# Reordering block products in a one-core hybrid layer: P2 moved ahead of P6

## The chip, the core and the metric

The kernel runs on one core of one Trainium2 chip. The metric is the device time of one execution in microseconds (us): the median of three runs before the change was 349.57 us (348.91 to 350.58). Profiled times come from one further execution, which the hardware profiler recorded.

Engines are called by the profile's names: PE does matmuls, PEld loads the stationary operand of a matmul, DVE is the vector engine, ACT the scalar engine, POOL the third elementwise engine (which here also starts some transfers), SP the engine that starts most transfers.

## The reference

One layer over 256 tokens of width 1024, batch 1. After a modulated RMS norm, one wide projection gives thirteen pieces: attention queries, keys, values and gate (`qa, ka, va, za`), the same for a recurrent memory (`qm, km, vm, zm, om` and two small gates), and two output gates:

```
h = _rmsnorm(x, norm_w) * (1 + scale) + shift
(qa, ka, va, za, qm, km, vm, zm, om, ig, fg, ga, gm) = jnp.split(h @ w_in, SPLIT_IDX, axis=-1)
ya = (ya * jax.nn.silu(za)) @ w_att_proj
hm = jax.nn.sigmoid(heads(om, ML_HEADS)) * hm
ym = (merge(hm) * jax.nn.silu(zm)) @ w_ml_proj
y = jax.nn.sigmoid(ga) * ya + jax.nn.sigmoid(gm) * ym
return x + gate * (y @ w_out)
```

Only four of the projections matter here: `vm` (the memory's values), `om` (its output gate), `zm` and `ga`. Each is a product of the 256x1024 matrix h with a 1024x1024 piece of `w_in`. Every order in which they are computed gives the same values.

## The kernel before, in words

**Matmul in three passes.** Every fp32 operand is split into a high part and a low rest, and each product is three matmuls: high by high, high by low, low by high. For the weights `split` (from L508) does it for one group at a time: ACT casts the raw weights to `wh` (L515), DVE subtracts to get `wl` (L519). Both live in rings of five buffers (`HB = 5`), and `split(g + 4)` is written in the loop turn of group g. So the cast of group g+4 has to wait until PE has finished group g-1, and ACT and DVE can be at most four groups ahead of PE.

**Groups.** PE works through a fixed list of groups, `place`. A whole group of `zm` (L1178 to L1180) is 12 matmuls 512 wide, a whole group of `ga` (L1185 to L1188) is 24 matmuls 256 wide. `zm` and `ga` have eight groups each, in two halves; `zm1.2` below is the third group of the second half.

**Block products.** `vm` and `om` are computed as 2x2 block matrices with seven products instead of eight (`PRODUCTS`, L51), in the order P1, P5, P3, P2, P6, P7, P4. Each product is two half groups of 6 matmuls 512 wide (L1161 to L1163). The seven products of one name share two banks of the accumulator memory (tiles called `aux`): P1, P2, P6 and P7 go to bank 0, P5, P3 and P4 to bank 1. Some add to what stands in the bank, some start it anew; P2 is added on top of P1, and **P6 starts bank 0 anew**. So whatever P2 completed has to be read out first:

- `ev_block(name, "P2")` calls `block_done(name, 0, 0, ...)`. For `om` that is one copy on ACT (L818, `omt<-aux`). For `vm` it is a cast on ACT (L822, `vaug<-aux`) and then a subtraction on DVE that reads the bank once more (L823, `vml<-aux,vaug`).
- P5 is copied out by ACT (L843), P6 by two instructions on DVE (L845, L846), P7 by two (L849, L850), P4 by one (L854); each of the last three is followed by a cast or a sigmoid on ACT (L822 or L818), and for `vm` by L823 on DVE.

These read-outs are written in the loop turn behind the last group of a product, after that turn's `split`. ACT and DVE do their work strictly in the order written, so a read-out stands behind the cast and the subtraction of the group four places ahead.

**Transfers.** The weights of a product come as a 1 MB block into one of seven raw buffers, started by SP as soon as a buffer is free. Products that need a sum of two weight blocks get the second block added by a transfer that accumulates, started by POOL three groups ahead (`block_sum`, L768).

**What sets the order.** The string `MIXED` (L54) is read letter by letter. V and O take the next product of `vm` and `om` (two half groups), z and g the next group of `zm` and `ga`. Nothing else is scheduled: the order of the instructions on each engine is the order in which the loop over `place` writes them:

```
pi = ended.get(g)
if g + A < NG:
    split(g + A, hooks_between.get(g, []))
    release(cons.get(g + A, []))
while pending:
    block_done(*pending.pop(0))
if block and pi != C["om", 6]:
    ev_block(chunks[pi]["name"], chunks[pi]["product"])
...
EV[pc["name"]](mmt[pi], pc["half"])
```

Groups are counted from the start of `place`; the first half group of `vm`'s P1 is 44.

Of the kernel before, what the change touches and what calls it, by code (L numbers as in the profile page):

```python
# [50 lines left out]
PRODUCTS = (("P1", (0, 0), 0, True), ("P5", (0, 0), 1, True), ("P3", (1, 1), 1, False), ("P2", (1, 0), 0, False),  # L51
            ("P6", (0, 0), 0, True), ("P7", (1, 1), 0, False), ("P4", (0, 0), 1, True))
BLOCK_SUMS = dict(P1=(0, 1), P5=(1, 1), P6=(1, 0), P3=(0, 1))
MIXED = "VzzzOzVzVzOVzVOzOOgVgOgVgOgggg"  # L54
W_PIECES = ((0, 512), (512, NR), (512, 1024), (1024, NR))


# [13 lines left out]
def tile_hybrid(ctx: ExitStack, tc: tile.TileContext, x, c, params2, w_row, w_va, ada_mod, ada_gate,  # L71
# [282 lines left out]
    for i, ch in enumerate(chunks):  # L354
        if ch["name"] == "ga" and ch["half"] == 0:
            whole = {name: [(C[name, hf], kp) for hf in range(2) for kp in range(4)] for name in ("ga", "zm")}
            whole.update({name: [(C[name, j], kp) for j in range(7) for kp in range(2)] for name in ("vm", "om")})
            for what in MIXED:
                name = dict(g="ga", z="zm", V="vm", O="om")[what]
# [895 lines left out]
```

## Time and profile before

| | before |
|---|---|
| median of 3 runs | 349.57 us |
| the profiled execution, its own time | 350.07 us |
| span from first to last instruction in it | 348.2 us |
| PE busy | 340.3 us (98%) |
| DVE busy | 276.8 us (79%) |
| ACT busy | 229.0 us (66%) |
| POOL busy | 84.5 us (24%) |

Busy time is the sum of an engine's instructions. A line of the timeline gives the start and the duration of an instruction in us from the start of the span, then engine, source line, operation, what it writes and reads, and, in brackets, how long its engine sat idle before it and which instruction released it. Matmuls are pipelined, so the next one starts well before the one before it has ended; how fast PE advances is read from one start to the next.

### The profile page before, as it was taken

Reading aid. Unit: us, or ns where it says so; the run is one execution under the profiler, and the core shown is the slowest. Engines: PE = TensorE matmul, PEld = TensorE weight load, DVE = VectorE, ACT = ScalarE, POOL = GpSimd, SP = SyncE. Lnnn points to the kernel's source line nnn. Section 1 sums busy time; section 2 is a strip of 40 time slices with the busy share of each in tenths; the row PEclk is TensorE's granted clock in tenths of the full one; section 3 lists DMA queues with packets and bytes.
Section 4 is the critical chain, followed back from the end, with each engine's and each line's share of the span. In section 5 each row is a group of like instructions: output and inputs, shape, how many; then the busy total and the mean of one; then the engine's idle time right before and its main releaser. Section 6 shows DMA issues by size and latency. Waiting matters only on the chain.

```text
span 348.2 us, 6229 instructions
## 1 busy us (share of the span) xinstructions
PE 340.3 (98%) x2408; PEld 318.3 (91%) x2408; DVE 276.8 (79%) x420; ACT 229.0 (66%) x355; POOL 84.5 (24%) x83
## 2 busy tenths in 40 slices
PE   7999999999999999999999999998999999999996
PEld 7787889999999999999998888777999999999995
DVE  5999996978995979776997778797796677759952
ACT  4868779799787676766747586675766554726410
POOL 4600002843201736554031332521000102000000
PEclk9999999999999999999999999999999999999999
DMA  7999999978481597283896999999997039160011
GB/s 267 420 414 413 418 417 422 311 285 354 148 337 62 179 361 253 70 320 151 284 266 176 232 149 256 263 242 262 391 350 272 0 124 360 64 243 0 2 60 62
DMA packets 30909, 84.09 MB, mean 241 GB/s; under 512 B 3224, under 2 KB 5152, under 8 KB 30240
## 3 DMA queue, kind: packets, MB, share of 16 engines
q1 hardware_dynamic: 26376, 74.78, 57.9%
q0 software_dynamic: 4352, 8.39, 13.9%
q10 hardware_dynamic: 152, 0.53, 0.4%
q8 instruction: 19, 0.31, 0.3%
q14 instruction: 10, 0.08, 0.1%
HBM read 82.43 MB, written 1.25 MB: 240 GB/s over the span
## 4 chain that ended last, share of the span: by engine, by line
PE 94%; DMA 2%; ACT 1%; DVE 1%; issue 1%; SPq 0%; ACTq 0%; DVEq 0%
PE mm L1187 15%; PE mm L1185 15%; PE mm L1188 15%; PE pm L202 13%; PE mm L1180 4%; PE mm L1179 4%; PE mm L1178 4%; PE aux L1161 4%; PE aux L1162 4%; PE aux L1163 4%; PE mm L1171 3%; DMA adat<-in_ada_mod_dram 2%; PE aux L671 1%; PE aux L709 1%; PE mm L1198 1%; PE mm L1200 1%
## 5 line engine op out<-in xcount | busy, mean ns | idle before, releaser
L519 DVE TENSOR_TENSOR wl<-raw,wh 128x1024 fp32r<-128x1024 f32 (+1 forms) x104 | 126.5, 1229 | 36.6 <-ACT wh L515 35.9
L515 ACT CAST wh<-raw 128x1024 fp32r<-128x1024 f32 (+1 forms) x112 | 112.1, 1017 | 31.2 <-PE mm L1187 15.1
L1185 PE MATMUL mm<-hTh,wh 128*128 128x256 f32 x320 | 90.0, 281 | 0.0
L1187 PE MATMUL mm<-hTl,wh 128*128 128x256 f32 x320 | 88.9, 278 | 0.0
L1188 PE MATMUL mm<-hTh,wl 128*128 128x256 f32 x320 | 88.9, 278 | 0.0
L1187 PEld LDWEIGHTS mm<-hTl,wh 128*128 128x128 f32 x320 | 60.4, 189 | 0.2
L1185 PEld LDWEIGHTS mm<-hTh,wh 128*128 128x128 f32 x320 | 60.1, 188 | 0.2
L1188 PEld LDWEIGHTS mm<-hTh,wl 128*128 128x128 f32 x320 | 60.2, 188 | 0.0
L768 POOL DMA_DIRECT2D raw<-in_w_in_dram x16 | 19.4, 1212 | 49.9 <-DVE wl L519 38.6
L1178 PE MATMUL mm<-wh,hTh 128*128 128x344 f32 (+1 forms) x80 | 28.0, 350 | 0.0
L1180 PE MATMUL mm<-wh,hTl 128*128 128x344 f32 (+1 forms) x80 | 27.7, 346 | 0.0
L1179 PE MATMUL mm<-wl,hTh 128*128 128x344 f32 (+1 forms) x80 | 27.7, 346 | 0.0
L519 POOL TENSOR_TENSOR wl<-raw,wh 128x1024 fp32r<-128x1024 f32 x8 | 20.0, 2527 | 15.8 <-ACT wh L515 15.8
L187 ACT CAST wrh<-raw 128x512 fp32r<-128x512 f32 (+1 forms) x24 | 18.2, 761 | 8.0 <-DMA raw<-in_w_row_dram 7.9
L192 DVE TENSOR_TENSOR wrl<-raw,wrh 128x512 fp32r<-128x512 f32 (+1 forms) x26 | 20.4, 812 | 1.1 <-ACT wrh L187 1.1
L202 PE MATMUL pm<-wrh,hTh 128*128 128x512 f32 x64 | 19.9, 392 | 0.4 <-ACT hTh L172 0.4
L202 PE MATMUL pm<-wrh,hTl 128*128 128x512 f32 x64 | 19.8, 391 | 0.0
L202 PE MATMUL pm<-wrl,hTh 128*128 128x512 f32 x64 | 19.0, 395 | 0.0
L1188 PE MATMUL mm<-yah,wl 128*128 128x256 f32 x64 | 17.7, 276 | 0.0
L1185 PE MATMUL mm<-yah,wh 128*128 128x256 f32 x64 | 17.7, 276 | 0.0
L1187 PE MATMUL mm<-yal,wh 128*128 128x256 f32 x64 | 17.7, 276 | 0.0
L1185 PE MATMUL mm<-ymh,wh 128*128 128x256 f32 x64 | 17.7, 276 | 0.0
(252 smaller groups left out, 773.4 us busy)
## 6 DMA issues: line engine op xcount, KB each, us to landing
raw<-in_w_in_dram SPq DMA_DIRECT2D x30, 1024.0 KB, 7.0
adat<-in_ada_mod_dram SPq DMA_DIRECT2D x16, 512.0 KB, 8.7
raw<-in_w_in_dram POOLq DMA_DIRECT2D x16, 512.0 KB, 8.5
raw<-in_w_va_dram SPq DMA_DIRECT2D x6, 688.0 KB, 9.3
raw<-in_ada_gate_dram SPq DMA_DIRECT2D x4, 1024.0 KB, 10.0
raw<-in_w_att_proj_dram SPq DMA_DIRECT2D x4, 1024.0 KB, 7.2
raw<-in_w_ml_proj_dram SPq DMA_DIRECT2D x4, 1024.0 KB, 7.2
raw<-in_w_out_dram SPq DMA_DIRECT2D x4, 1024.0 KB, 5.5
```

The lines of the kernel that those rows point to most:

```text
L187: copy(wsp[k][0][:, c0:c1], wrow[k][:, c0:c1])
L192: e.tensor_tensor(l[:, cs], wrow[k][:, cs], h[:, cs].bitcast(F32), op=OP.subtract)
L202: nc.tensor.matmul(pm[ch][:, t], a[:, k, t * 128:(t + 1) * 128], b[:, cs], start=k == 0 and i == 0, stop=k == KT - 1 and i == 2)
L515: nc.scalar.copy(h, w)
L519: e.tensor_tensor(l, w, h.bitcast(F32), op=OP.subtract)
L768: nc.gpsimd.dma_start(rawt[li][:, ks], w_block(ch["name"], *BLOCK_SUMS[ch["product"]])[:, ks], accum_op=OP.add)
L1178: nc.tensor.matmul(o, a, wh[:, kk], start=first, stop=False)
L1179: nc.tensor.matmul(o, a, wl[:, kk], start=False, stop=False)
L1180: nc.tensor.matmul(o, b, wh[:, kk], start=False, stop=last)
L1185: nc.tensor.matmul(o, wh[:, kk, cs], sh_[:, k], start=first and i % 2 == 0, stop=False, skip_group_check=True)
L1187: nc.tensor.matmul(o, wh[:, kk, cs], sl_[:, k], start=False, stop=False, skip_group_check=True)
L1188: nc.tensor.matmul(o, wl[:, kk, cs], sh_[:, k], start=False, stop=last and i % 2 == 1, skip_group_check=True)
```

## The change

Only the string that sets the order differs:

```diff
-MIXED = "VzzzOzVzVzOVzVOzOOgVgOgVgOgggg"
+MIXED = "VzzzOzVzVzVOzVOOzgOVgVgOgOgggg"
```

The groups that come out of it, from 58 on (before 58 and after 83 the two lists are the same; .0 and .1 are the two halves of a product):

| groups | before | now |
|---|---|---|
| 58, 59 | om P5 | vm P2 |
| 60, 61 | vm P2 | om P5 |
| 62 | zm1.2 | zm1.2 |
| 63, 64 | vm P6 | vm P6 |
| 65, 66 | om P3 | om P3 |
| 67 to 69 | zm1.3, om P2.0, om P2.1 | om P2.0, om P2.1, zm1.3 |
| 70 to 72 | om P6.0, om P6.1, ga0.0 | ga0.0, om P6.0, om P6.1 |
| 73, 74 | vm P7 | vm P7 |
| 75 | ga0.1 | ga0.1 |
| 76, 77 | om P7 | vm P4 |
| 78 | ga0.2 | ga0.2 |
| 79, 80 | vm P4 | om P7 |
| 81 | ga0.3 | ga0.3 |
| 82, 83 | om P4 | om P4 |

No instruction is added or taken away on PE, DVE, ACT, POOL or SP; they stand in another order. On PE, at the end of `om`'s P2 (its last three matmuls, which write the bank `aux_2314` from `hTh` and `hTl`), before, P6 writes the same bank next, from `hsum`:

```order
L1161 MATMUL aux_2314<-wh_2554,hTh_70 128x512
L1162 MATMUL aux_2314<-wl_2555,hTh_70 128x512
L1163 MATMUL aux_2314<-wh_2554,hTl_71 128x512
L1161 MATMUL aux_2314<-wh_2568,hsum_2206 128x512
L1162 MATMUL aux_2314<-wl_2569,hsum_2206 128x512
L1163 MATMUL aux_2314<-wh_2568,hsum_2206 128x512
```

and now the last group of `zm` follows (12 matmuls of which three are shown, then the 24 of ga0.0, and only then P6):

```order
L1161 MATMUL aux_2314<-wh_2542,hTh_70 128x512
L1162 MATMUL aux_2314<-wl_2543,hTh_70 128x512
L1163 MATMUL aux_2314<-wh_2542,hTl_71 128x512
L1178 MATMUL mm_2410<-wh_2554,hTh_70 128x512
L1179 MATMUL mm_2410<-wl_2555,hTh_70 128x512
L1180 MATMUL mm_2410<-wh_2554,hTl_71 128x512
```

Two whole groups have come between P2 and P6 on PE.

On ACT, which reads `vm`'s and `om`'s P2 out of the bank (L822 `vaug<-aux` and L818 `omt<-aux`; one `wh<-raw` is the cast of one group, L843 the read-out of `om`'s P5, L764 that of `zm`), from the middle of the stretch, before:

```order
L843 COPY omt<-aux 128x512
L515 CAST wh<-raw 128x1024 x2
L822 CAST vaug<-aux 128x2x256
L515 CAST wh<-raw 128x1024 x4
L822 CAST vaug<-vmt 128x2x256
L515 CAST wh<-raw 128x1024 x2
L764 ACTIVATE zmt<-mm 128x2x512
L515 CAST wh<-raw 128x1024 x2
L818 ACTIVATE omt<-aux 128x512
L515 CAST wh<-raw 128x1024 x3
L818 ACT_TABLE_LOAD
```

and now:

```order
L822 CAST vaug<-aux 128x2x256
L515 CAST wh<-raw 128x1024 x2
L843 COPY omt<-aux 128x512
L515 CAST wh<-raw 128x1024 x4
L822 CAST vaug<-vmt 128x2x256
L515 CAST wh<-raw 128x1024 x3
L818 ACTIVATE omt<-aux 128x512
L515 CAST wh<-raw 128x1024
L764 ACTIVATE zmt<-mm 128x2x512
L515 CAST wh<-raw 128x1024 x4
L818 ACT_TABLE_LOAD
```

The read-out of `vm`'s P2 comes two casts sooner, that of `om`'s P2 one cast sooner and ahead of `zm`'s; the table load ahead of `om`'s first sigmoid comes one cast later.

On DVE, from the read-out of P7 of `vm` on (L849, L850), before, `om`'s P7 (`omt`) goes ahead of `vm`'s P4 (L854 `vmt<-aux,vmt`):

```order
L849 TENSOR_TENSOR omt<-aux,omt 128x512
L850 TENSOR_TENSOR omt<-omt 128x512
L519 TENSOR_TENSOR wl<-raw,wh 128x1024 x3
L854 TENSOR_TENSOR vmt<-aux,vmt 128x512
L519 TENSOR_TENSOR wl<-raw,wh 128x1024
L823 TENSOR_TENSOR vml<-vmt,vaug 128x512
L519 TENSOR_TENSOR wl<-raw,wh 128x1024
L854 TENSOR_TENSOR omt<-aux,omt 128x512
```

and now it follows it:

```order
L854 TENSOR_TENSOR vmt<-aux,vmt 128x512
L519 TENSOR_TENSOR wl<-raw,wh 128x1024
L823 TENSOR_TENSOR vml<-vmt,vaug 128x512
L519 TENSOR_TENSOR wl<-raw,wh 128x1024 x2
L849 TENSOR_TENSOR omt<-aux,omt 128x512
L850 TENSOR_TENSOR omt<-omt 128x512
L519 TENSOR_TENSOR wl<-raw,wh 128x1024 x2
L854 TENSOR_TENSOR omt<-aux,omt 128x512
```

The two read-outs have changed places, with the subtractions of the weights around them shared out anew.

## The prediction

> **What bounds the kernel now.** I read the page's busy times and chain first, then the list of what PE waited for, and then the timeline of PE at the two waits that lie in the stretch the change touches.
>
> ```profile
> PE 340.3 (98%) x2408; PEld 318.3 (91%) x2408; DVE 276.8 (79%) x420; ACT 229.0 (66%) x355; POOL 84.5 (24%) x83
> PE 94%; DMA 2%; ACT 1%; DVE 1%; issue 1%; SPq 0%; ACTq 0%; DVEq 0%
> PE aux L1161 <- ACT omt L818: 1.8, 1, 1.8
> PE warm L231 <- POOL ident masks.py:199: 1.4, 1, 1.4
> PE xps L267 <- ACT diag L250: 0.7, 1, 0.7
> PE pm L202 <- ACT hTh L172: 0.4, 1, 0.4
> PE aux L1161 <- DVE vml L823: 0.3, 1, 0.3
> ```
>
> PE is busy for 98% of the span and makes up 94% of the chain that ended last. So only what makes PE stand still counts, and the list of its waits is short: three at the start, where nothing changes, and two on L1161, the first matmul of a block product. One waits for ACT's copy of `om`'s P2 (L818), the other for DVE's subtraction in the read-out of `vm`'s P2 (L823). These are the two P6 that must not start bank 0 anew before P2 has been read out of it.
>
> ```profile
> 220.37 0.39 PE L1163 MATMUL aux<-wh,hTl 128*128 128x512 f32 x1
> ...
> 223.09 0.39 PE L1180 MATMUL mm<-wh,hTl 128*128 128x512 f32 x1
> 223.77 0.50 PE L1161 MATMUL aux<-wh,hsum 128*128 128x512 f32 x1 [0.29 <-DVE vml L823]
> ...
> 226.62 0.39 PE L1161 MATMUL aux<-wh,hsum 128*128 128x512 f32 x1
> ...
> 234.55 0.39 PE L1163 MATMUL aux<-wh,hTl 128*128 128x512 f32 x1
> 236.70 0.50 PE L1161 MATMUL aux<-wh,hsum 128*128 128x512 f32 x1 [1.76 <-ACT omt L818]
> ...
> 239.57 0.28 PE L1185 MATMUL mm<-hTh,wh 128*128 128x256 f32 x1
> ...
> 242.40 0.40 PE L1161 MATMUL aux<-wh,hsum 128*128 128x512 f32 x1
> ```
>
> The rows are, in order: the last matmul of `vm`'s P2, the last of zm1.2, the first of `vm`'s P6, the first of `om`'s P3, the last of `om`'s P2, the first of `om`'s P6, the first of ga0.0, and the first of `vm`'s P7. Between 226.62 and 234.55 PE runs freely for 35 matmuls, so one takes (234.55 - 226.62) / 35 = 0.2266 us.
>
> **What the two waits cost.** From the last matmul of zm1.2 to the first of `om`'s P3 are 13 steps (12 matmuls of P6 lie between): 226.62 - 223.09 = 3.53 us against 13 x 0.2266 = 2.95, so 0.58 us are lost. From the last of `om`'s P2 to the first of ga0.0 are 13 steps too: 239.57 - 234.55 = 5.02 against 2.95, so 2.07 us. Together 2.65 us. The lower bound is the idle time alone that the rows in brackets show, 0.29 + 1.76 = 2.05 us: it leaves out that the bar of the last matmul runs on for 0.39 us where a free stream would have started the next after 0.23, and that the first matmul behind a wait takes 0.50 us. The upper bound is the idle time of the weight loads in the same stretch, which stood 2.2 and 0.7 us for the same two releasers:
>
> ```profile
> L1161 PEld LDWEIGHTS aux<-wh,hsum 128*128 128x128 f32 x12 | 2.2, 187 | 3.3 <-ACT omt L818 2.2 <-DVE vml L823 0.7
> ```
>
> That makes 2.9 us. I take 2.65, because only it counts from start to start. The Trainium skill (Trainium Kernel Development and Optimization, section Performance Expectations) calls matmul busy time a bad metric, since matmuls are pipelined, and names the busy share of LDWEIGHTS as a good one. By that rule the sum would be nearer to 2.9 than to 2.05; the trace agrees so far that the matmul bars of 0.39 us overlap at a spacing of 0.23.
>
> **Does the new order remove them?** The read-outs themselves:
>
> ```profile
> 220.80 1.06 ACT L515 CAST wh<-raw 128x1024 fp32r<-128x1024 f32 x1 [0.24 <-PE aux L1163]
> 221.76 0.57 ACT L822 CAST vaug<-aux 128x512 fp32r<-128x512 f32 x1
> 220.59 2.52 DVE L519 TENSOR_TENSOR wl<-raw,wh 128x1024 fp32r<-128x1024 f32 x2 [0.20 <-ACT wh L515]
> 223.03 0.68 DVE L823 TENSOR_TENSOR vml<-aux,vaug 128x512 fp32r<-128x512 f32 x1
> 234.17 1.98 ACT L515 CAST wh<-raw 128x1024 fp32r<-128x1024 f32 x2
> 236.05 0.60 ACT L818 ACTIVATE omt<-aux 128x512 f32<-128x512 f32 x1
> ```
>
> In both cases ACT first casts the group four places ahead, whose ring buffer comes free only as P2 ends, and then reads the bank; for `vm` DVE follows, behind two subtractions of weights. From the start of P2's last matmul to the end of the read-out: `vm` 223.03 + 0.68 - 220.37 = 3.34 us, `om` 236.05 + 0.60 - 234.55 = 2.10 us. The same instructions stand ahead of the read-outs in the new order, so I keep these times. Room that they get now, from the start of P2's last matmul to P6: for `vm` 1 + 12 (`om`'s P5) + 12 (zm1.2) = 25 matmuls, 25 x 0.2266 = 5.66 us; for `om` 13 matmuls of 0.2266 (zm1.3 among them) and the 24 matmuls of ga0.0. A whole group of `ga` takes 2.83 us: ga0.0 begins at 239.57, and `vm`'s P7 follows at 242.40. That is 2.95 + 2.83 = 5.78 us. Left over: 2.3 us for `vm` and 3.7 us for `om`. Both waits should go whole. If the cover went (a read-out later by more than that), the wait would come back, microsecond for microsecond.
>
> **What the change moves besides, at no cost as I see it.** No engine gets an instruction more, so the sum has only the two terms above. Other read-outs keep their distance from the matmul that needs the bank: `om`'s P3 adds to bank 1 after P5's copy, with zm1.2 and P6 of `vm` between as cover, 12 + 12 matmuls or 5.4 us, against one cast and a copy, 1.06 + 0.57. `vm`'s P4 and `om`'s P7 start 11 and 6 places behind the P6 read-out that they need. The weights for six half groups in a row (63 to 68) are the first thing that could become late: ACT needs 0.99 us a group (1.98 for two), DVE 1.18 (2.35 for two, below), PE 6 x 0.2266 = 1.36. DVE loses its margin wherever read-outs stand between. The tightest place I find is ga0.3, group 81:
>
> ```profile
> 243.54 1.28 ACT L818 ACT_TABLE_LOAD   x1
> 244.84 1.06 ACT L818 ACTIVATE omt<-omt 128x1024 f32<-128x1024 f32 x1
> 252.21 2.35 DVE L519 TENSOR_TENSOR wl<-raw,wh 128x1024 fp32r<-128x1024 f32 x2
> 256.29 0.28 PE L1185 MATMUL mm<-hTh,wh 128*128 128x256 f32 x1
> 240.00:262.00 22.00, 22.00 (x144) 20.04 (x143) 19.00 (x21) 15.78 (x17) 0.00 (x0) 1.00 1.03 346
> ```
>
> Its `wl` is the first of the two in the third row, ready at about 252.21 + 1.22 = 253.43, and PE starts it at 256.29: a lead of 2.86 us. Now `om`'s P6 comes one half group later, and with it the block of table load and sigmoid on ACT (1.28 + 1.06 us), so ACT and DVE have some 1.36 us less to recover in before group 81. The lead shrinks to about 1.5 us (an estimate from these rows). It stays positive, so this costs nothing; without that cover it would be up to 1 us. The last row is the stage by engines: columns are the stretch, its length, then PE, PEld, DVE, ACT and POOL. DVE is busy for 19.0 of 22 us: busy, but not the bound.
>
> Transfers: ga0.0's weights are needed two groups sooner. Before, their load went out behind the last subtraction of `vm`'s P2:
>
> ```profile
> 209.69 2.54 DVE L519 TENSOR_TENSOR wl<-raw,wh 128x1024 fp32r<-128x1024 f32 x2
> 215.13 0.37 SPq L414 DMA_DIRECT2D raw<-in_w_in_dram  x1
> raw<-in_w_in_dram SPq DMA_DIRECT2D x1, 1024.0 KB, 11.3
> raw<-in_w_in_dram SPq DMA_DIRECT2D x1, 1024.0 KB, 16.8
> 228.18 1.06 ACT L515 CAST wh<-raw 128x1024 fp32r<-128x1024 f32 x1 [0.30 <-PE aux L1163]
> 235.15 1.22 POOL L768 DMA_DIRECT2D raw<-in_w_in_dram  x1 [1.96 <-DVE wl L519]
> raw<-in_w_in_dram POOLq DMA_DIRECT2D x1, 512.0 KB, 11.8
> 253.67 1.05 ACT L515 CAST wh<-raw 128x1024 fp32r<-128x1024 f32 x1 [0.56 <-ACT wh L515]
> 255.81 1.22 DVE L519 TENSOR_TENSOR wl<-raw,wh 128x1024 fp32r<-128x1024 f32 x1
> ```
>
> P2's subtractions are now those at places 58 and 59, done at 209.69 + 2.54 = 212.2 (first row), so the load starts 2.9 us sooner than at 215.13, and lands after 11.3 us at about 223.5. The cast at place 70 ran at 228.18, now some 0.6 us sooner: 4 us to spare. SP's other loads keep their order. POOL's small cast L839 moves ahead of two of the accumulating transfers, whose data is needed some 12 places on.
>
> **Sum.** Against the profiled execution's own time: 350.07 - 2.65 = 347.42 us. The median of the runs shown lies 0.50 below that execution, so 349.57 - 2.65 = 346.92, **347.0 us** rounded, 0.75% faster. With the bounds 2.05 and 2.9: 347.5 and 346.7.
>
> **Rivals.**
>
> *The weights come late at ga0.3.* For it speaks that the lead halves there, that DVE is busy 86% of the stage, and that the waits of before gave ACT and DVE time to catch up. Against it: the lead is estimated above zero, and no wait for `wh` or `wl` stands in the list of before. If I misjudge the lead by 2.5 us, PE waits 1 us there and the gain is 1.65: 347.9 us; with a second such place 348.5.
>
> *ACT and DVE set the pace anyway.* Then PE, freed of two waits, meets the same time again at the next groups whose weights aren't ready: 349.6 us. Against it: ACT's cast at 220.80 and 228.18 waits for PE, not PE for it. That the order doesn't do what it says (a read-out of P2 still late) ends here too, but needs it to be 2.3 and 3.7 us later than measured.
>
> *A transfer for `om`'s P4 lands late, and it gets slower.* The accumulating transfer behind `om`'s P6 went out at 235.15 and took 11.8 us; it now starts a group later in the program, at about 236.5, and lands at 248.3, while the second half of P4 is not moved. Its cast ran at 253.67, now at about 253.67 - 2.65 = 251.0: 2.7 us of slack, and then a lead over PE of about 3.5 us: its `wl` was ready at 255.81 + 1.22 = 257.03, and PE came to it at 256.29 + 2.83 + 1.36 = 260.48. So PE stops from a landing time of 11.8 + 2.7 + 3.5 = 18 us on, and the kernel is slower by over 0.5% from 18 + 2.65 + 1.75 = 22.4 us on; the longest that I found in this stretch is 16.8. At 24 us it costs 6 and the time is 349.57 - 2.65 + 6 = 352.9 us.
>
> **How the numbers follow.** Chances: forecast 0.76, late weights 0.10, pace set elsewhere 0.10, late transfer 0.04. The forecast's own range is 346.2 to 347.8 (the bounds and half the spread of the runs before). To leave out no more than 2 in 10 the range must reach over the late weights: 346.0 to 349.2. What a measurement of this kernel can tell from no change is about 0.5%, 1.75 us, so faster means below 347.8. Faster: nearly all of the forecast and a third of the late weights, 0.74. Slower: the late transfer and a little scatter, 0.05. Within 0.5%: the rest, 0.21.
>
> **What would show it.** In the changed profile the list of PE's waits should hold no L1161 row; the step at `om`'s P6 should be 0.12 us behind ga0.0's last matmul. A PE row waiting for DVE's `wl` (L519) near ga0.3 speaks for late weights; ACT's cast idle behind a transfer at `om`'s P4 for the last rival. The prediction is wrong if PE's waits go and the span does not get shorter by 2 us or more.

## The result and the profile after

The changed kernel takes 346.74 us (median of 6 runs, 346.28 to 347.70), against 349.39 us for the kernel before beside it (6 runs). The ratio is 0.9927, with a 95% interval of 0.9905 to 0.9948. It is faster by 2.65 us; the forecast was 2.65 us and 347.0 us. The interval allows 1.8 to 3.3 us, so that the medians meet the forecast to the hundredth is luck.

The page of the changed kernel, its busy times and its chain, and the whole list of what PE waited for:

```profile
PE 339.0 (98%) x2408; PEld 318.2 (92%) x2408; DVE 276.6 (80%) x420; ACT 228.7 (66%) x355; POOL 85.7 (25%) x83
PE 98%; ACT 1%; POOL 0%; DVE 0%; issue 0%; POOLq 0%
PE warm L231 <- POOL ident masks.py:199: 1.4, 1, 1.4
PE xps L267 <- ACT diag L250: 0.7, 1, 0.7
```

Both rows of L1161 are gone; what is left lies at the start. Note that PE's busy share is 98% as before: it says nothing of the gain.

The two profiled spans differ by 348.2 - 344.5 = 3.7 us, which is more than the medians do. To see what belongs to the change I count the stretch from the first matmul of `vm`'s P1, where the first product of the reordered list begins, to the start of the program's last matmul. Timeline of PE, kernel before:

```profile
183.24 0.40 PE L1161 MATMUL aux<-wh,hTh 128*128 128x512 f32 x1
344.49 0.28 PE L1200 MATMUL mm<-wh,yl 128*128 128x256 f32 x1
```

and after:

```profile
182.23 0.40 PE L1161 MATMUL aux<-wh,hTh 128*128 128x512 f32 x1
340.83 0.28 PE L1200 MATMUL mm<-wh,yl 128*128 128x256 f32 x1
```

That is 161.25 us before and 158.60 after: 2.65 us from the change. The other 1.01 us passed ahead of anything that the change touches, in the first 183 us; over the profiled executions of all kernels here that first part ended between 182.17 and 183.84 us.

The read-outs in the changed kernel, with the PE rows that bound them (last matmul of `vm`'s P2, first of its P6, then the same for `om`; between them stand the rows of ACT and DVE):

```profile
216.64 0.39 PE L1163 MATMUL aux<-wh,hTl 128*128 128x512 f32 x1
218.03 0.57 ACT L822 CAST vaug<-aux 128x512 fp32r<-128x512 f32 x1
219.30 0.68 DVE L823 TENSOR_TENSOR vml<-aux,vaug 128x512 fp32r<-128x512 f32 x1
222.31 0.39 PE L1161 MATMUL aux<-wh,hsum 128*128 128x512 f32 x1
...
230.24 0.39 PE L1163 MATMUL aux<-wh,hTl 128*128 128x512 f32 x1
228.90 0.62 ACT L822 CAST vaug<-vmt 128x512 fp32r<-128x512 f32 x1 [1.26 <-DVE vmt L846]
229.42 2.95 ACT L515 CAST wh<-raw 128x1024 fp32r<-128x1024 f32 x3
232.28 0.58 ACT L818 ACTIVATE omt<-aux 128x512 f32<-128x512 f32 x1
236.01 0.40 PE L1161 MATMUL aux<-wh,hsum 128*128 128x512 f32 x1
```

`vm`: read out 219.98 - 216.64 = 3.34 us after the start of P2's last matmul, with 222.31 - 216.64 = 5.67 us of room. `om`: 232.86 - 230.24 = 2.62 us, with 5.77 us of room. Neither P6 meets its read-out any more.

### The profile page after: what moved, and what is told of

It reads as the page before. It is cut to its first block, busy times and chain, and to the rows that moved or that the text cites. A ratio compares the mean times of both kernels' runs of the same rounds, so it can differ in the third digit from the quotient of the medians.

```text
span 344.5 us, 6230 instructions
## 1 busy us (share of the span) xinstructions
PE 339.0 (98%) x2408; PEld 318.2 (92%) x2408; DVE 276.6 (80%) x420; ACT 228.7 (66%) x355; POOL 85.7 (25%) x83
## 4 chain that ended last, share of the span: by engine, by line
PE 98%; ACT 1%; POOL 0%; DVE 0%; issue 0%; POOLq 0%
PE mm L1188 15%; PE mm L1185 15%; PE mm L1187 15%; PE pm L202 13%; PE mm L1178 4%; PE mm L1180 4%; PE mm L1179 4%; PE aux L1161 4%; PE aux L1162 4%; PE aux L1163 4%; PE mm L1171 3%; PE xps L267 1%; PE mm L1200 1%; PE aux L709 1%; PE mm L1199 1%; PE mm L1198 1%
## 5 line engine op out<-in xcount | busy, mean ns | idle before, releaser
L519 POOL TENSOR_TENSOR wl<-raw,wh 128x1024 fp32r<-128x1024 f32 x8 | 20.0, 2531 | 15.8 <-ACT wh L515 10.5
```

The costliest lines, as they stand in the source:

```text
L519: e.tensor_tensor(l, w, h.bitcast(F32), op=OP.subtract)
```

## The experiments

The theory: PE sets the pace, and the two waits for the read-out of P2 are the whole difference. The main rival: ACT and DVE set the pace, so that time saved at a wait is given back further on. "The stretch" is the one counted above. Nine more kernels were run. Seven differ from the two above in the order alone; the other two are the changed kernel with copies on ACT that nobody reads.

### Only vm's P2 moved

```diff
-MIXED = "VzzzOzVzVzOVzVOzOOgVgOgVgOgggg"
+MIXED = "VzzzOzVzVzVOzVOzOOgVgOgVgOgggg"
```

> The order of before, with only vm's P2 and om's P5 exchanged. The stretch is counted from the first matmul of vm's P1 to the start of the program's last matmul: 344.49 - 183.24 = 161.25 us before, 340.83 - 182.23 = 158.60 in the changed kernel. Theory (PE's two waits for the read-out of P2 are the whole difference): the wait on DVE's L823 goes, the one on ACT's L818 of 1.8 us stays; stretch 161.25 - 0.58 = 160.67 us, time 0.6 below before, 348.8. Rival (ACT and DVE set the pace and the gain came from the order as a whole): a wait for wl or a longer one at om's P6; stretch 161.2 or nearer to 158.6.

Measured: stretch 343.65 - 182.95 = 160.70 us, 0.55 less than before. Median 349.30 us (12 runs) against 349.48 (29 runs), ratio 0.9982 (0.9962 to 1.0003). In PE's list behind the start only one row is left:

```profile
PE aux L1161 <- ACT omt L818: 1.8, 1, 1.8
```

The wait on L823 has gone alone and has taken its own share with it, as the theory says. By the run times alone, 0.55 us could not have been told from nothing.

### Only om's P2 and P6 moved

```diff
-MIXED = "VzzzOzVzVzOVzVOzOOgVgOgVgOgggg"
+MIXED = "VzzzOzVzVzOVzVOOzgOVgOgVgOgggg"
```

> The order of before, with only om's P2 one group sooner and its P6 behind ga0.0; vm's P2 and the P4/P7 pair stay as before. Theory: the wait on L818 goes, the 0.3 us wait on L823 stays; stretch 161.25 - 2.07 = 159.18 us, time 2.1 below before, 347.3. Rival (pace): stretch 160 or more, with PE waiting for wl near ga0.3.

Measured: stretch 341.39 - 182.17 = 159.22 us, 2.03 less than before; median 347.29 us (9 runs), ratio 0.9940 (0.9917 to 0.9963). The row that remains is the other one:

```profile
PE aux L1161 <- DVE vml L823: 0.3, 1, 0.3
```

0.55 and 2.03 make 2.58 of the 2.65 us: the two parts add up. No PE wait for `wl` appears near ga0.3.

### Only vm's P4 and om's P7 exchanged

```diff
-MIXED = "VzzzOzVzVzOVzVOzOOgVgOgVgOgggg"
+MIXED = "VzzzOzVzVzOVzVOzOOgVgVgOgOgggg"
```

> The order of before, with only vm's P4 and om's P7 exchanged. Theory: no wait of PE hangs on them, both waits on L1161 stay as before; stretch 161.25 us within 0.1, time 349.4. Rival (the read-outs' new distribution on ACT and DVE is worth something by itself): stretch shorter by 0.3 us or more.

Measured: median 349.58 us (12 runs), ratio 0.9998 (0.9978 to 1.0019), both waits as before, 1.8 and 0.3 us. But the stretch of the profiled execution was 345.45 - 182.65 = 162.80 us, 1.55 more than expected. The stages of this execution around `om`'s P6 (columns: stretch, its length, busy time with count of PE, PEld, DVE, ACT and POOL, granted clock of PE, share and GB/s of the DMA engines), and the two matmuls on either side of the pause:

```profile
234.00:236.00 2.00, 0.40 (x2) 0.00 (x0) 1.37 (x3) 2.00 (x3) 1.22 (x1) 1.00 1.10 262
236.00:237.00 1.00, 0.84 (x4) 0.71 (x5) 1.00 (x1) 0.10 (x1) 0.00 (x0) 1.00 1.11 262
237.00:238.00 1.00, 1.00 (x4) 0.80 (x3) 0.06 (x1) 0.00 (x0) 0.00 (x0) 0.56 1.10 262
238.00:240.00 2.00, 2.00 (x6) 1.52 (x6) 0.58 (x1) 1.04 (x1) 0.00 (x0) 0.50 1.09 261
240.00:241.00 1.00, 1.00 (x7) 0.86 (x6) 0.65 (x1) 0.19 (x1) 0.00 (x0) 0.73 1.08 266
241.00:242.00 1.00, 1.00 (x12) 1.00 (x11) 0.10 (x1) 0.87 (x1) 0.00 (x0) 1.00 1.09 262
```

```profile
234.01 0.39 PE L1163 MATMUL aux<-wh,hTl 128*128 128x512 f32 x1
236.16 0.50 PE L1161 MATMUL aux<-wh,hsum 128*128 128x512 f32 x1 [1.76 <-ACT omt L818]
```

The granted clock falls to 0.50 behind the pause and comes back at about 240.5. The lost clock, added up over the rows, is 0.44 + 2 x 0.50 + 0.27 = 1.71 us at full speed, which covers the 1.55. So the exchange itself is worth nothing that these runs can tell, as the median says, but a pause can cost more than its length. The last experiment takes that up.

### The whole change without that exchange

```diff
-MIXED = "VzzzOzVzVzVOzVOOzgOVgVgOgOgggg"
+MIXED = "VzzzOzVzVzVOzVOOzgOVgOgVgOgggg"
```

> The changed order without the exchange of vm's P4 and om's P7. Theory: as the changed kernel, stretch 158.60 us within 0.1, no PE wait on L1161, time 346.7. Rival (vm's P4 sooner is needed for the gain, or eats part of it): stretch off by 0.3 us or more either way.

Measured: stretch 342.39 - 183.79 = 158.60 us, no wait of PE in it; median 347.00 us (9 runs), ratio 0.9929 (0.9904 to 0.9953). `vm`'s P4 two places sooner is neither needed for the gain nor does it eat any.

### One group instead of two between om's P2 and P6

```diff
-MIXED = "VzzzOzVzVzVOzVOOzgOVgVgOgOgggg"
+MIXED = "VzzzOzVzVzVOzVOOzOgVgVgOgOgggg"
```

> The changed order with om's P6 ahead of ga0.0 again, so that only one whole group, zm1.3, stands between om's P2 and P6: room 13 x 0.2266 = 2.95 us against a read-out of 1.94 us measured in the changed kernel (232.28 + 0.58 - 230.92) and 2.10 before. Theory (what counts is room against read-out): no wait, stretch 158.60 us within 0.1, time 346.7. Rival (it takes the three places, one group is not enough, as it wasn't for vm's P2): a wait on L818 at om's P6 of 0.3 us or more, stretch 158.9 or more.

Measured: stretch 340.90 - 182.30 = 158.60 us, no wait; median 346.51 us (4 runs), ratio 0.9917 (0.9902 to 0.9931). The 1.94 us in the expectation was counted from a wrong row: P2's last matmul in the changed kernel starts at 230.24, so the read-out there took 2.62 us. The same shows here:

```profile
230.31 0.39 PE L1163 MATMUL aux<-wh,hTl 128*128 128x512 f32 x1
...
232.35 0.58 ACT L818 ACTIVATE omt<-aux 128x512 f32<-128x512 f32 x1
...
233.26 0.39 PE L1161 MATMUL aux<-wh,hsum 128*128 128x512 f32 x1
```

232.93 - 230.31 = 2.62 us of read-out in 2.95 us of room. It held with 0.33 us to spare, where the expectation had 1 us. One whole group is enough for `om`, whose read-out ends on ACT; it was not enough for `vm`, whose read-out goes on to DVE and takes 3.34 us.

### Nothing between vm's P2 and P6

```diff
-MIXED = "VzzzOzVzVzOVzVOzOOgVgOgVgOgggg"
+MIXED = "VzzzOzVzVzOzVVOzOOgVgOgVgOgggg"
```

> The order of before with zm1.2 ahead of vm's P2, so that nothing stands between vm's P2 and P6. Theory: the wait on L823 grows by the cover taken away, one whole group of 2.72 us; the read-out took 3.34 us from the start of P2's last matmul, so about 3.3 us are lost there instead of 0.58; om's 2.07 stay; stretch 161.25 + 2.7 = 163.95 us, time 352.1. Rival (ACT and DVE set the pace, the wait lets them catch up and is given back further on): stretch under 163 us.

Measured: median 353.59 us (4 runs, 352.18 to 354.49), ratio 1.0116 (1.0081 to 1.0150); stretch 347.80 - 182.19 = 165.61 us, 4.36 more than before where 2.7 were expected. PE's waits:

```profile
PE aux L1161 <- DVE vml L823: 3.0, 1, 3.0
PE aux L1161 <- ACT omt L818: 1.8, 1, 1.8
```

The wait grew from 0.3 to 3.0 us, by the whole group of cover, and nothing was given back: the rival, under 163 us, falls. The 1.66 us too many are the clock again, behind the long pause (by the clock column 0.43 + 2 x 0.50 + 0.28 = 1.71 us at full speed are lost):

```profile
226.00:227.00 1.00, 1.00 (x4) 0.80 (x3) 0.00 (x0) 0.00 (x0) 0.74 (x1) 0.57 1.11 205
227.00:228.00 1.00, 1.00 (x4) 0.71 (x4) 0.00 (x0) 0.20 (x1) 0.46 (x1) 0.50 1.13 205
228.00:229.00 1.00, 1.00 (x4) 0.80 (x3) 0.12 (x1) 0.85 (x1) 0.00 (x0) 0.50 1.13 240
229.00:230.00 1.00, 1.00 (x5) 0.81 (x4) 1.00 (x1) 0.00 (x0) 0.00 (x0) 0.72 1.09 262
```

The one execution of the four with a mean granted clock of 1.0 took 352.18 us, the 352.1 expected; the others had 0.990 to 0.995.

### Two and five added copies on ACT

In the changed kernel, in the loop turn of group 75, n copies of 1024 columns into a spare buffer (n = 2 and 5):

```diff
-    T["A"] = {}
+    T["A"] = {}; at(75, lambda: [nc.scalar.copy(hl.tile([128, 4, 256], F32, name="spare", tag="scr", bufs=2),
+                                                hTh[:, 0:4].bitcast(F32)) for _ in range(n)])
```

> The changed kernel with two added ACT copies of 1024 columns (about 0.95 us each, of hTh into a spare buffer that nobody reads) in the loop turn of group 75, right ahead of the cast of group 80. In the changed kernel ACT stood idle for 1.66 us before vm's next cast there, and wl of ga0.3 was ready 1.21 us ahead of PE. Theory (PE sets the pace and the lead is real): 1.9 us of added work fit into 1.66 + 1.21 = 2.87 us; stretch 158.60 us within 0.1, time 346.7. Rival (ACT and DVE are the pace, the lead is an artefact): stretch longer by up to 1.9 us, 160.5.

> As the kernel with two added copies, with five: 4.75 us of added ACT work against 2.87 us of room. Theory: PE waits about 1.9 to 2.2 us for wl at vm's P4 and ga0.3 (groups 80 and 81); stretch 160.5 to 160.8 us, time 348.8. Rival (the lead is larger than read from the rows, ACT catches up over the neighbours): stretch under 159.5. Rival (ACT is the pace): stretch 163.3.

Measured with two: stretch 340.88 - 182.28 = 158.60 us, no wait of PE; median 346.49 us (4 runs), ratio 0.9920 (0.9904 to 0.9937). ACT's rows:

```profile
245.92 1.99 ACT L1075 COPY spare<-hTh 128x1024 f32<-128x1024 f32 x2
247.82 1.05 ACT L515 CAST wh<-raw 128x1024 fp32r<-128x1024 f32 x1
248.76 0.62 ACT L822 CAST vaug<-vmt 128x512 fp32r<-128x512 f32 x1
```

These 1.99 us of ACT's time cost nothing: they fill the 1.66 us in which ACT had stood idle ahead of the row of L822, and a part of the lead. Measured with five: stretch 343.20 - 182.73 = 160.47 us, 1.87 more, 0.03 under the low end of what the theory gave; median 348.34 us (8 runs), ratio to the kernel before 0.9974 (0.9964 to 0.9985). Now PE waits for ACT's cast and for what DVE makes of it:

```profile
246.38 4.83 ACT L1075 COPY spare<-hTh 128x1024 f32<-128x1024 f32 x5
PE aux L1162 <- DVE wl L519: 0.8, 1, 0.8
PE aux L1161 <- ACT wh L515: 0.3, 1, 0.3
```

Both waits fall in group 80, the second half of `om`'s P7; the expectation calls that group `vm`'s P4, which is its name in the order of before. ga0.3 behind it has no row in the list. So PE sets the pace in this stage, with about 2.9 us of ACT's time in hand at this place: of the 4.75 us of the five copies about 2.9 fit, and the rest cost its own length, 1.87.

### One long pause alone

```diff
-MIXED = "VzzzOzVzVzVOzVOOzgOVgVgOgOgggg"
+MIXED = "VzzzOzVzVzOzVVOOzgOVgVgOgOgggg"
```

> The changed kernel with zm1.2 ahead of vm's P2, so that vm's P2 and P6 touch, and om's P6 free: one pause of PE, of 3.0 us by the list of waits, instead of two. In the kernel with both pauses the stretch was 165.61 us, 1.66 more than the 163.95 expected, and the granted clock fell to 0.50 for some 3.4 us behind the long pause; three of its four executions had a mean clock of 0.990 to 0.995. Theory (a pause of about 3 us makes the clock fall behind it more often than not, one of 2 us seldom, one under 1 us never): stretch 158.60 + 3.3 = 161.9 us where the clock stays, 1.5 to 1.7 us more where it falls; most executions at a mean clock of 0.995 and about 350.1 + 1.6 us, the rest at 1.0 and 350.1. Rival (the fall of the clock has nothing to do with the length of the pause): a mean clock of 0.998 or more in nine of ten executions, as in the kernel before, and a median of 350.1.

Measured: median 351.73 us (12 runs, 350.15 to 354.11), ratio 1.0056 (1.0033 to 1.0079). Ten of the 12 executions had a mean granted clock of 0.990 to 0.995; the two at 0.999 took 350.15 and 350.25 us, which is the 350.1 expected for a clock that stays. The stretch was 347.30 - 183.84 = 163.46 us: 161.9 and 1.56 for the clock. PE around the pause, and the stages:

```profile
223.70 0.39 PE L1163 MATMUL aux<-wh,hTl 128*128 128x512 f32 x1
227.08 0.65 PE L1161 MATMUL aux<-wh,hsum 128*128 128x512 f32 x1 [3.00 <-DVE vml L823]
227.53 0.63 PE L1162 MATMUL aux<-wl,hsum 128*128 128x512 f32 x1
227.96 0.63 PE L1163 MATMUL aux<-wh,hsum 128*128 128x512 f32 x1
...
231.05 0.39 PE L1162 MATMUL aux<-wl,hsum 128*128 128x512 f32 x1
231.28 0.39 PE L1163 MATMUL aux<-wh,hsum 128*128 128x512 f32 x1
```

```profile
227.00:228.00 1.00, 0.92 (x3) 0.73 (x4) 0.02 (x1) 0.00 (x0) 0.00 (x0) 0.63 1.13 205
228.00:229.00 1.00, 1.00 (x4) 0.81 (x3) 0.00 (x0) 0.00 (x0) 0.95 (x1) 0.50 1.12 207
229.00:230.00 1.00, 1.00 (x4) 0.80 (x3) 0.00 (x0) 0.10 (x1) 0.26 (x1) 0.50 1.13 205
230.00:231.00 1.00, 1.00 (x4) 0.77 (x3) 0.02 (x1) 0.95 (x1) 0.00 (x0) 0.66 1.16 219
```

Behind the pause one matmul takes 227.96 - 227.53 = 0.43 us from start to start, at 231 again 0.23. The rival (length doesn't matter) falls. Note that PE's busy share reads 1.00 while it runs at half speed; only the clock column and the spacing show it.

## Why the prediction was right

- **What the two waits cost.** Counted from start to start, 0.58 + 2.07 = 2.65 us; the stretch got shorter by 2.65. The two runs that moved one part each measured 0.55 and 2.03. Neither bound would have served as the value: PE's idle time, 2.05 us, leaves out what is lost at the edges of a pause, and the idle time of the weight loads, 2.9, reads too large.
- **Whether the new order removes them.** For `vm` the step holds to the hundredth: 3.34 us of read-out in 5.67 of room. For `om` the step "the same instructions stand ahead of the read-outs, so I keep these times" was wrong: 2.62 us, not 2.10. ACT was behind. Its cast in `vm`'s P6 read-out, which waits 1.26 us for DVE, now starts only 230.24 - 228.90 = 1.34 us ahead of P2's last matmul, since zm1.3 no longer stands between; in the kernel before it was 234.55 - 230.49 = 4.06 us:

```profile
230.49 0.62 ACT L822 CAST vaug<-vmt 128x512 fp32r<-128x512 f32 x1 [1.25 <-DVE vmt L846]
```

  Three casts in a row (229.42, 2.95 us) then end 2.13 us behind the start of that matmul, where the last cast used to end 1.60 us behind it. The slack was 3.15 us, not 3.7. It decided nothing here; in the kernel with one group in between it left 0.33 us.
- **The lead at ga0.3.** Estimated at 1.5 us. Timeline of the changed kernel:

```profile
242.67 1.28 ACT L818 ACT_TABLE_LOAD   x1 [1.30 <-DVE omt L846]
...
250.20 2.35 DVE L519 TENSOR_TENSOR wl<-raw,wh 128x1024 fp32r<-128x1024 f32 x2
...
252.63 0.28 PE L1185 MATMUL mm<-hTh,wh 128*128 128x256 f32 x1
```

  The first of the two subtractions is ready at 250.20 + 1.22 = 251.42, so the lead is 1.21 us. It is positive, as the step needed, but that the estimate came so near is in part luck. The table load used to stand 256.29 - 243.54 = 12.75 us ahead of ga0.3 and now stands 252.63 - 242.67 = 9.96 us ahead of it: it moved by 2.79 us, a whole group of `ga`, and not by the 1.36 us of a half group that the step counted. The lead fell by only 1.65 us, because DVE now makes the weights of three groups instead of four between the read-out of `om`'s P6 and those of ga0.3, and one group takes it 1.18 us. Added ACT work used the lead up about where the rows said it would.
- **Transfers.** ga0.0's load started at 211.25 on a timeline that runs 1.01 us ahead, so at 212.26 by that of before: 212.2 was predicted. It landed after 6.9 us instead of 11.3. The accumulating transfers behind `om`'s P6 took 10.5 us in the median. No cast of ACT waited for a transfer in the stretch, so nothing was late.
- **The sum.** Against the profiled execution it gave 347.42; that of the changed kernel took 346.51 us. The difference of 0.91 us comes from the start of the program, which was 1.01 us shorter there and on which the change has no bearing. The median is the fairer check: 347.0 (the sum gave 346.92) against 346.74. One price of a rival is added wrongly: two places of 1 us each would leave 0.65 us of the gain, 348.9 and not 348.5; the range covers both.
- **What it did not see.** The rivals had no falling clock among them. It adds to the price of a pause in some executions only, and for pauses of 2 us in few of them, so it moved neither of the two medians that the prediction compares.

## What to carry to other kernels

Where one engine is busy all the time, list its few waits, and price each from instruction start to instruction start, against the free spacing nearby; idle time alone reads too small. An accumulator bank that is started anew should be reused no sooner than its read-out takes, counted from the last matmul into it, with the work that stands ahead on the reading engines included; more room than that buys nothing. Before crediting such a gain, check that the feeding engines have a lead at every later group, and measure the effect over the stretch that changed, since the start of the program alone scattered by 1.7 us here.

## What was not expected of the hardware

A pause of PE can cost half its clock for some 3.4 us afterwards. With a pause of 3.0 us by the list of waits (3.4 from the last start to the next) this happened in 10 of 12 executions, with one more pause of 1.8 us in 3 of 4, and it cost about 1.6 us in each of the two that were profiled. With pauses of 1.8 us at most, in the kernel before and the two variants that keep `om`'s wait, a mean clock of 0.995 appeared in 4 of 81 executions; one of these, profiled, shows the fall right behind the pause. In kernels with no pause over 0.8 us behind the program's start, 39 of 40 executions stayed at 0.998 or more; the one at 0.994 was not profiled, so its cause stays open.

In the three profiled falls the clock went down 0.96, 0.72 and 0.19 us behind the end of the pause (one pause of 1.76 us, two of 3.0 us) and stayed at 0.50 for 3.41 us. The trace's clock records put these moments on a grid: from the first record of an execution to the fall pass 232.11, 218.45 and 221.87 us, which are 68, 64 and 65 steps of 3.413 us. Where a pause lies on this grid doesn't decide alone: in the profiled execution of the kernel before, the pause of 1.76 us stood at the same place, from 0.20 to 0.71 of a step, as in the execution that fell (0.20 to 0.72), and the clock stayed at 1.00. Why one fell and the other did not stays open.

The Trainium skill (TensorE: Matmul & The Clock Gate, section "What's actually happening") lets the clock fall after at least one idle window of about 3.4 us that runs freely. The length of the slow time and the grid fit such a window. The falls do not fit a window that is idle throughout: PE was idle for 1.76 us ahead of one of them (2.15 us between two starts, 234.01 to 236.16) and for 3.0 us ahead of the other two, each time less than the window.
